# A list scheduler's rules in a two-layer diffusion backbone: which buffer, which rank, which order at the start

## The chip, the cores and the metric

The kernel runs on one core of a Trainium2 chip. The engines of a core each take their instructions in order: TensorE (PE, with its weight loads as PEld), VectorE (DVE), ScalarE (ACT), GpSimd (POOL) and SyncE (SP), which here only issues DMAs; ScalarE issues some too. The metric is the device time of one execution in microseconds.

## The reference

The input is 256 context tokens and 256 latent tokens of 1024 channels, in float32. Two layers change them; in each, a modulated RMS norm comes before an FFN, four token mixers (gated DeltaNet, Hyena, Mamba-2 SSD, GLA) and a second FFN. What matters of it:

```python
def pre_norm(t, gain, m, i):
    return modulate(rms_norm(t, gain), m[..., 3 * i, :], m[..., 3 * i + 1, :])

def swiglu(h, w_up, w_down):
    a, g = jnp.split(h @ w_up, 2, axis=-1)
    return (jax.nn.silu(a) * g) @ w_down
...
    for layer in range(DEPTH):
        mx = (cond_x @ w_ada[layer] + b_ada[layer]).reshape(b, 1, N_MOD, D_MODEL)
        mc = (cond_c @ w_ada[layer] + b_ada[layer]).reshape(N_MOD, D_MODEL)
        x = x + 0.5 * mx[..., 2, :] * swiglu(pre_norm(x, nw[0], mx, 0), ffn_up[layer, 0], ffn_down[layer, 0])
        yc, yx = token_mix(pre_norm(xc, nw[1], mc, 1), pre_norm(x, nw[1], mx, 1), w_in[layer], ...)
        x = x + mx[..., 5, :] * yx
        x = x + 0.5 * mx[..., 8, :] * swiglu(pre_norm(x, nw[2], mx, 2), ffn_up[layer, 1], ffn_down[layer, 1])
    return rms_norm(x, final_norm)
```

The context (xc) goes the same way with mc. The Hyena mixer needs filters that depend on weights alone: a small FFN, times a window, then a Fourier transform.

## The kernel before

**Tiling.** Activations lie with channels on the 128 partitions and tokens along them, as 128x512 tiles. Products are taken in a split form: a weight chunk `raw` is split into a high part `wh` (ScalarE, in the start GpSimd) and a rest `wl` (VectorE), an activation into `hh` and `hl`, and each product is three matmuls: wh with hh, wl with hh, wh with hl. `raw`, `wh` and `wl` have three buffers each.

**Norms.** A norm sums squares, turns the mean into a root by a chain of ten short VectorE steps on 128x4 values (`ms`, then `rq`, `rt`, `ru` by turns), spreads it to all partitions by a matmul with `rq`, and then makes for each of eight channel blocks `u` (VectorE, x times the root), `hh` (ScalarE) and `v` (GpSimd, two halves), and `hl` = v - hh (VectorE).

**Filters.** `G_unit` multiplies the output weights `hywo` of the filter FFN with its hidden values and windows them into `hSD`; `G_dft` transforms them into tiles `gA`, `gB` and a row `gn`, which SP stores to DRAM tensors `gdr`: all of gA, rows 1 to 127 of gA once more, gn and gB. Four of the norms (`norm_G`, L2153) mix these transforms with their own TensorE work, so that TensorE has something to do while the root is made. The modulation sums (`aa`, from weights `aw`) run on VectorE in between, over the whole kernel.

**Buffers.** `slot` (L609) gives a 128x512 tile of one pool of 34: u, v, hSD, gA, gB, gn, qkv, aw and more come out of it.

**Order.** Nothing is issued as the code is written. `body` runs against `Stand`, which records each operation with its engine, its dependences and a key: the sum of TensorE's time up to there (`self.t`), less an offset. `Plan` then walks through modelled time: of an engine's ready operations the one with the smallest key is next, and when an operation needs a new tile, the plan also picks which buffer of the pool it gets. `build` issues all operations in the plan's sequence, each buffer being a pool of its own with one place, and the tile framework adds the semaphore waits: an operation that writes into a buffer waits for the real end of the last one that used it. All planned instructions bear one line, L573, the call in `build`. `order` (L2445 on) makes the plan with a margin of 300 ns between engines.

Two calls in the kernel code, `manual_schedule(engines)` and `high_priority(offset)`, are recorded without effect in before: `manual_schedule` does nothing, and `high_priority` adds an offset of zero. They stand around `start()` (the loads, the first norm and the first product, for which all engines but SP were named), around the whole of `norm_G` (TensorE), in `wchunk` (L674, the splits of weight chunks) and in `gdn_proj`.

Of the kernel before, what the change touches and what calls it, by code (L numbers as in the profile page):

```python
# [10 lines left out]
F32 = mybir.dt.float32  # L11
# [125 lines left out]

class Op:  # L140

    __slots__ = ("n", "eng", "name", "args", "kw", "key", "deps", "left", "succ", "occ", "dur", "new", "tiles", "func", "ready", "dma", "start", "port")
# [7 lines left out]
class Stand:  # L150
# [3 lines left out]
    def __init__(self, nc):  # L154
        self.real, self.shadow = nc, _bacc.Bacc("TRN2", target_bir_lowering=False, num_devices=1)
        self.ops, self.tiles, self.hist, self.dr = [], {}, {}, set()
        self.t, self.off, self.pe_last, self.maker = 0.0, [0.0], {}, {}
        self.lane = ""
        for a, e in self.ENG.items():
            setattr(self, a, self.Engine(self, e))  # L160

# [22 lines left out]

    @contextlib.contextmanager
    def manual_schedule(self, engines=None):
        yield

    @contextlib.contextmanager
    def high_priority(self, offset=0):  # L190
        self.off.append(self.off[-1])
        yield
        self.off.pop()

# [35 lines left out]
    def note(self, eng, name, args, kw):  # L230
        if name == "preload_act_table_set":
            return Note()
        o = Op()
        o.n, o.eng, o.name, o.args, o.kw = len(self.ops), eng, name, args, kw
        o.dma = name == "dma_start"
        o.deps, o.succ, o.new, o.tiles = {}, [], None, []
        aps = [x for x in list(args) + list(kw.values()) if isinstance(x, bass.AP)]
        o.func = None
        for x in list(args) + list(kw.values()):
            if isinstance(x, type(AF.Copy)):  # L240
                o.func = x
        for i, x in enumerate(aps):
            tn, w = x.tensor.name, i == 0
            if tn in self.tiles:
                b = self.box(x)
                if tn not in o.tiles:
                    o.tiles.append(tn)
                    if tn not in self.hist:
                        assert w, (tn, name)
                        o.new, self.maker[tn] = tn, o.n  # L250
                    else:

                        o.deps.setdefault(self.maker[tn], -1)
            elif tn in self.dr:
                b = self.dbox(x)
            else:
                continue
            self.access(o, tn, w, b, tn in self.dr)
            if w and eng == "PE":
                p = self.pe_last.get(tn)  # L260
                if p is not None:
                    o.deps[p] = max(o.deps.get(p, 0), 0)
                self.pe_last[tn] = o.n
        for tn in o.tiles:
            self.tiles[tn][5] += 1
        self.cost(o, aps)
        o.key = self.t - self.off[-1]
        if eng == "PE":
            self.t += o.occ / 1e3
        self.ops.append(o)  # L270
        return Note()
# [86 lines left out]
class Plan:  # L358
# [10 lines left out]
    def run(self):  # L369
        st, ops = self.st, self.ops  # L370
# [39 lines left out]
        pend = {e: [] for e in engs}  # L410
        avail = {e: {} for e in engs}
        ft = {e: 0.0 for e in engs}
        table, dmaf, port = "S", 0.0, {"DVE": 0.0, "POOL": 0.0}
        G, posted = [], set()
        waiters = {}

# [12 lines left out]
        while G:  # L429
            t, e = heapq.heappop(G)  # L430
            posted.discard((t, e))
            if t < ft[e]:
                post(ft[e], e)
                continue
            while pend[e] and pend[e][0][0] <= t:
                o = ops[heapq.heappop(pend[e])[1]]
                c = st.tiles[o.new][0] if o.new else None
                heapq.heappush(avail[e].setdefault(c, []), (keys[o.n], o.n))
            best = None
            for c, h in avail[e].items():  # L440
                if not h:
                    continue
                k, n = h[0]
                if c is not None:

                    fr = free[c]
                    nf = sum(1 for f in fr if f[0] <= t)
                    i = nextpos[c]
                    if not nf or (pos[n] > i and slack[c][i:pos[n]].min() < 1):

                        m = self.order[c][nextpos[c]] if nextpos[c] < len(self.order[c]) else None
                        if nf and m is not None and m != n and (keys[m], m) in h:
                            k, n = keys[m], m
                        else:
                            later = [f[0] for f in fr if f[0] > t]
                            if later:
                                post(min(later), e)
                            waiters.setdefault(c, set()).add(e)
                            continue
                o = ops[n]  # L460
                if e == "ACT":
                    ta = table_of(o)
                    if ta and ta != table:
                        k += self.swap
                if best is None or k < best[0]:
                    best = k, n, c
            if best is None:
                if pend[e]:
                    post(max(pend[e][0][0], ft[e]), e)
                continue  # L470
            _, n, c = best
            o = ops[n]
            h = avail[e][c]
            if h[0][1] == n:
                heapq.heappop(h)
            else:
                h.remove((keys[n], n))
                heapq.heapify(h)
            if c is not None:
                fr = free[c]  # L480
                f = max((x for x in fr if x[0] <= t), key=lambda x: x[0])
                fr.remove(f)
                self.slot[o.new] = f[1]
                done_new.add(n)
                slack[c][nextpos[c]:pos[n]] -= 1
                l = self.order[c]
                while nextpos[c] < len(l) and l[nextpos[c]] in done_new:
                    nextpos[c] += 1
                    for x in waiters.pop(c, ()):
                        post(t, x)  # L490
            occ, dur = o.occ, o.dur
            if e == "ACT":
                ta = table_of(o)
                if ta and ta != table:
                    table = ta
                    occ, dur = occ + 1283, dur + 1283
            o.start = t
            if o.port:
                x = 0.7 * max(0.0, min(port["POOL" if e == "DVE" else "DVE"] - t, dur))
                occ, dur = occ + x, dur + x  # L500
                port[e] = t + dur
            ft[e] = t + occ
            if o.dma:
                b = max(t + occ, dmaf)
                dmaf = b + dur / 230.0
                end = dmaf + 2300
            else:
                end = t + dur
            seq.append(n)
            n_done += 1  # L510
            for s in o.succ:
                x = ops[s]
                if x.deps[n] < 0:
                    r = t + 1
                elif x.deps[n] == 0 and x.eng == e:
                    r = t + occ
                elif x.eng == e and not o.dma:
                    r = end if e != "PE" else t + occ
                else:
                    r = end + self.LAT[x.eng] + self.margin  # L520
                x.ready = max(x.ready, r)
                x.left -= 1
                if not x.left:
                    push(x)
            for tn in o.tiles:
                left[tn] -= 1
                endt[tn] = max(endt[tn], end)
                if not left[tn]:
                    c2 = st.tiles[tn][0]
                    free[c2].append((endt[tn] + 60, self.slot[tn]))  # L530
                    for x in waiters.pop(c2, ()):
                        post(max(endt[tn] + 60, ft[x]), x)
            post(ft[e], e)
# [46 lines left out]
class Kern:  # L580
# [44 lines left out]
        self.nc.sync.dma_start(s[:, t:], d[:, t:])  # L625
        return s

    def small(self, shape, s="sm", dt=F32, bufs=8):
        return self.pt.tile(list(shape), dt, name=self.nm(s), tag="sm%d" % int(np.prod(shape[1:])), bufs=bufs)

    def psum(self, tag="mm", shape=(128, 512)):
# [1811 lines left out]


def order(st):  # L2445
    plan = Plan(st, {}, 300.0, 8.0)
    if plan.stuck:
        raise RuntimeError("no order found")
    return plan


def body(nc, tc, I, O):
    from contextlib import ExitStack
    with ExitStack() as es:
        K = Kern(nc, tc, I, es)
        with tc.manual_schedule(engines={mybir.EngineType.PE, mybir.EngineType.DVE, mybir.EngineType.Activation, mybir.EngineType.Pool}):
            acts = K.start()
        K.ada_it, K.ada_done = K.ada(), (0, 1)
        with tc.issue_after(K.last_ld.ins):
# [58 lines left out]
```

## Time and profile before

| | us |
|---|---|
| median of three runs | 2789.42 |
| lowest and highest | 2787.28, 2791.71 |
| the profiled execution | 2792.31 |
| its span, first to last instruction | 2790.5 |
| TensorE busy, idle | 2656.2, 134.3 |
| VectorE, ScalarE, GpSimd busy | 1894.4, 1049.6, 360.4 |

The mean granted TensorE clock over the span is 0.976 of 2.4 GHz. The rows below come from the page of the profile, from lists of who waited for whom, from the chain of work that ended last (each piece is what released the next), from lists of instructions in order of time, and from busy times by stretch. In a list in order of time, the number in front is the start in us, the second the time until the end of the last instruction of the piece, and the brackets hold the idle time of the engine ahead of the piece and what ended it.

### The profile page before, as it was taken

The numbers are of one execution on the slowest core, as the hardware profiler recorded it, in microseconds if no ns is written. First come the engines' busy times: TensorE is split into PE (matmuls) and PEld (weight loads), VectorE is DVE, ScalarE is ACT, GpSimd is POOL, SyncE is SP. The second block draws the span as 40 slices with busy tenths as digits, with TensorE's granted clock in tenths as the row PEclk, the third lists the DMA queues.
The fourth block names the chain that finished last, engine by engine and source line by source line (L and its number), as shares of the span: only waits on it lengthen the run. The fifth ranks groups of instructions, "written<-read, shape, count | busy, mean of one in ns | idle before, by whom it ended". The sixth has DMA issues, their size and how long they took to land.

```text
span 2790.5 us, 40144 instructions
## 1 busy us (share of the span) xinstructions
PE 2656.2 (95%) x15131; PEld 2279.0 (82%) x15131; DVE 1894.4 (68%) x3783; ACT 1049.6 (38%) x1603; POOL 360.4 (13%) x439
## 2 busy tenths in 40 slices
PE   3999998899999999998999998999989999999998
PEld 2788876688989888886888877888868899999998
DVE  3978873679867565588637668376347988777555
ACT  1322222554433543233222223222237435644443
POOL 1200000201121243421000001000013012222000
PEclk7999999999999999999999998999989999999999
DMA  8655543243344233254534544344224445555454
GB/s 239 191 172 185 180 141 115 62 114 84 106 134 143 75 104 105 76 167 154 163 98 151 151 135 152 106 151 138 92 79 119 133 122 149 177 163 182 152 183 142
DMA packets 369698, 382.67 MB, mean 137 GB/s; under 512 B 43466, under 2 KB 317544, under 8 KB 369504
## 3 DMA queue, kind: packets, MB, share of 16 engines
q1 hardware_dynamic: 347568, 363.67, 43.1%
q10 hardware_dynamic: 21936, 16.44, 1.9%
q8 instruction: 119, 1.95, 0.3%
q14 instruction: 75, 0.61, 0.1%
HBM read 355.79 MB, written 24.25 MB: 136 GB/s over the span
## 4 chain that ended last, share of the span: by engine, by line
PE 86%; DVE 6%; DMA 5%; issue 1%; ACT 1%; SPq 1%; POOL 1%; ACTq 0%; DVEq 0%
PE pmm L573 74%; PE px L573 12%; DMA gdr<-gA 2%; DVE qkv L573 1%; DVE aa L573 1%; DVE wl L573 1%; SPq L573 1%; DMA gdr<-gn 1%; DVE xbc L573 1%; POOL bm L573 0%; DMA aw<-in_w_ada 0%; DVE x L573 0%; DMA win<-in_hywin 0%; DVE TC L573 0%; DVE u L573 0%
## 5 line engine op out<-in xcount | busy, mean ns | idle before, releaser
L573 PE MATMUL pmm<-hh,wh 128*128 128x512 f32 (+1 forms) x2464 | 895.9, 364 | 24.7 <-ACT hh L573 17.6
L573 ACT ACTIVATE wh<-raw 128x1024 fp32r<-128x1024 f32 (+1 forms) x480 | 501.5, 1046 | 1100.9 <-PE pmm L573 1044.4
L573 DVE TENSOR_TENSOR wl<-raw,wh 128x1024 fp32r<-128x1024 f32 (+1 forms) x486 | 600.7, 1237 | 462.1 <-ACT wh L573 437.0
L573 PE MATMUL pmm<-hh,wl 128*128 128x512 f32 (+1 forms) x2464 | 888.7, 361 | 1.6 <-DVE wl L573 1.5
L573 PE MATMUL pmm<-hl,wh 128*128 128x512 f32 (+1 forms) x2464 | 883.3, 360 | 5.2 <-DVE hl L573 5.2
L573 PEld LDWEIGHTS pmm<-hh,wh 128*128 128x128 f32 x2464 | 470.4, 191 | 99.7 <-ACT hh L573 18.5
L573 PEld LDWEIGHTS pmm<-hl,wh 128*128 128x128 f32 x2464 | 468.3, 190 | 74.4 <-DVE hl L573 5.9
L573 PEld LDWEIGHTS pmm<-hh,wl 128*128 128x128 f32 x2464 | 470.7, 191 | 67.9 <-DVE wl L573 2.1
L573 DVE SCALAR_TENSOR_TENSOR aa<-aw,cond,aa 128x256 f32<-128x256 f32 x896 | 374.0, 482 | 1.7 <-DMA aw<-in_w_ada 1.6
L573 PE MATMUL pmm<-ah,wh 128*128 128x512 f32 (+1 forms) x704 | 257.3, 366 | 0.6 <-DVE sil L573 0.6
L573 PE MATMUL pmm<-ah,wl 128*128 128x512 f32 (+1 forms) x704 | 255.6, 363 | 0.0
L573 PE MATMUL pmm<-al,wh 128*128 128x512 f32 (+1 forms) x704 | 255.6, 363 | 0.0
L573 PEld LDWEIGHTS pmm<-ah,wh 128*128 128x128 f32 x704 | 133.1, 189 | 24.4 <-issue 2.5
L573 PEld LDWEIGHTS pmm<-al,wh 128*128 128x128 f32 x704 | 133.0, 189 | 21.1 <-issue 0.4
L573 PEld LDWEIGHTS pmm<-ah,wl 128*128 128x128 f32 x704 | 133.1, 189 | 20.3
L573 POOL TENSOR_SCALAR v<-u,Am,mods 128x256 f32<-128x256 f32 x72 | 56.1, 795 | 514.7 <-DVE u L573 472.4
L573 PE MATMUL pmm<-wh,hh 128*128 128x256 f32 x416 | 120.2, 289 | 0.0
L573 PE MATMUL pmm<-wl,hh 128*128 128x256 f32 x416 | 119.3, 287 | 0.0
L573 PE MATMUL pmm<-wh,hl 128*128 128x256 f32 x416 | 118.8, 286 | 0.0
L573 PE MATMUL pmm<-yh,wh 128*128 128x512 f32 (+1 forms) x256 | 87.6, 343 | 0.0
L573 PE MATMUL pmm<-yl,wh 128*128 128x512 f32 (+1 forms) x256 | 86.3, 340 | 0.0
L573 PE MATMUL pmm<-yh,wl 128*128 128x512 f32 (+1 forms) x256 | 86.1, 337 | 0.0
(383 smaller groups left out, 3396.8 us busy)
## 6 DMA issues: line engine op xcount, KB each, us to landing
raw<-in_ffn_up SPq DMA_DIRECT2D x172, 512.0 KB
raw<-in_w_in SPq DMA_DIRECT2D x164, 512.0 KB
aw<-in_w_ada SPq DMA_DIRECT2D x288, 256.0 KB
raw<-in_ffn_down SPq DMA_DIRECT2D x80, 512.0 KB
raw<-in_w_branch SPq DMA_DIRECT2D x32, 512.0 KB
fe<-pk SPq DMA_DIRECT2D x42, 256.0 KB
raw<-in_w_out SPq DMA_DIRECT2D x16, 512.0 KB
pk<-pj ACTq DMA_DIRECT2D x26, 256.0 KB
```

Of the source, the lines that this page charges most:

```text
L573: getattr(engines[o.eng], o.name)(*[sub(a) for a in o.args], **{k: sub(v) for k, v in o.kw.items()})
```

## The change

The operations, their number and their sizes stay as they are. What changes is how the plan is made:

- `manual_schedule` takes effect: the operations of each named engine inside it are chained in the order in which the code states them. SP is now named too at `start()`, and after that block no operation gets a key below the TensorE time at its end (`floor`).
- `high_priority` lowers the key by 15 us (`lead`): the splits of weight chunks and the raw copies of `gdn_proj` rank that much earlier.
- A new tile gets the buffer that has been free longest, not the one that became free last.
- Of two dependent operations on one engine (DVE, ACT, POOL) the second may be planned as soon as the engine has taken the first (`occ`), not at its end.
- Each DMA queue has a modelled rate of its own, 290 B/ns for SP and 100 for ScalarE; before, both shared 230.
- The margin between engines is 200 ns, not 300, and small tiles have 6 buffers, not 8.

```diff
     def manual_schedule(self, engines=None):
+        self.strict = {NAMES[e]: None for e in engines}
         yield
+        if "SP" in self.strict:
+            self.floor = self.t
+        self.strict = {}
...
     def high_priority(self, offset=0):
-        self.off.append(self.off[-1])
+        self.off.append(self.off[-1] + self.lead)
...
+        if eng in self.strict:
+            if self.strict[eng] is not None:
+                o.deps.setdefault(self.strict[eng], -1)
+            self.strict[eng] = o.n
...
-        o.key = self.t - self.off[-1]
+        o.key = max(self.t - self.off[-1], self.floor)
...
                 fr = free[c]
-                f = max((x for x in fr if x[0] <= t), key=lambda x: x[0])
+                f = min(fr)
...
-                b = max(t + occ, dmaf)
-                dmaf = b + dur / 230.0
-                end = dmaf + 2300
+                b = max(t + occ, dmaf[e])
+                dmaf[e] = b + dur / (290.0 if e == "SP" else 100.0)
+                end = dmaf[e] + 2300
...
                 elif x.eng == e and not o.dma:
-                    r = end if e != "PE" else t + occ
+                    r = t + occ
...
-    def small(self, shape, s="sm", dt=F32, bufs=8):
+    def small(self, shape, s="sm", dt=F32, bufs=6):
...
-    plan = Plan(st, {}, 300.0, 8.0)
+    plan = Plan(st, {}, 200.0, 8.0)
...
-        with tc.manual_schedule(engines={mybir.EngineType.PE, mybir.EngineType.DVE, mybir.EngineType.Activation, mybir.EngineType.Pool}):
+        with tc.manual_schedule(engines={mybir.EngineType.PE, mybir.EngineType.DVE, mybir.EngineType.Activation, mybir.EngineType.Pool,
+                                         mybir.EngineType.SP}):
```

How it moves instructions, at three places. A row is an instruction with its tiles (a name, the number of the tile and a running number) and, in brackets, the semaphores that it waits for; DMAHW0 to 7 are those of DMAs.

VectorE in the norm ahead of the first FFN of layer 1 (norm_G(1,0), near 1680 us; x a token tile, px the spread root), before:

```order
L573 TENSOR_TENSOR u2679_14332<-x2092_10723,px2678_14318 128x512 [waits DMAHW1_49,PE_49]
L573 TENSOR_TENSOR u2680_14339<-x2093_10746,px2678_14318 128x512 [waits DMAHW7_49]
L573 TENSOR_TENSOR u2681_14349<-x2104_10782,px2678_14318 128x512
L573 TENSOR_TENSOR u2682_14354<-x2105_10805,px2678_14318 128x512
L573 TENSOR_TENSOR u2687_14363<-x2122_10838,px2678_14318 128x512 [waits DVE_49,Activation_49,Pool_49]
L573 TENSOR_TENSOR hl2684_14371<-v2685_14345,hh2683_14343 128x512
L573 TENSOR_TENSOR u2691_14383<-x2123_10863,px2678_14318 128x512
L573 TENSOR_TENSOR u2695_14391<-x2134_10889,px2678_14318 128x512 [waits DMAHW7_49]
L573 TENSOR_TENSOR u2699_14398<-x2135_10918,px2678_14318 128x512 [waits DMAHW6_49,DMAHW5_49,DMAHW4_49]
```

and of the change:

```order
L585 TENSOR_TENSOR u2679_14303<-x2092_10706,px2678_14285 128x512 [waits PE_49]
L585 TENSOR_TENSOR u2680_14306<-x2093_10729,px2678_14285 128x512
L585 TENSOR_TENSOR u2681_14315<-x2104_10776,px2678_14285 128x512
L585 TENSOR_TENSOR u2682_14321<-x2105_10796,px2678_14285 128x512
L585 TENSOR_TENSOR hl2684_14329<-v2685_14311,hh2683_14309 128x512 [waits Activation_49,Pool_49]
L585 MEMSET gB2674_14323 1x256 [waits Activation_49]
L585 TENSOR_TENSOR u2687_14343<-x2122_10831,px2678_14285 128x512
L585 TENSOR_TENSOR u2691_14353<-x2123_10850,px2678_14285 128x512
L585 TENSOR_TENSOR u2695_14361<-x2134_10885,px2678_14285 128x512
L585 TENSOR_TENSOR u2699_14370<-x2135_10902,px2678_14285 128x512
```

The eight u stand in nearly the same row; the four waits for DMAs are no longer there.

VectorE in the middle of the first FFN (near 430 us; hSD windowed filters, win the window, hyb a bias row), before:

```order
L573 COPY gn634_3679<-px633_3665 1x256 [waits DMAHW1_49,DMAHW2_49,DMAHW0_49,PE_49]
L573 TENSOR_TENSOR hSD642_3690<-px641_3681,win1_173 128x512 [waits DMAHW4_49,DVE_49,PE_49]
L573 MEMSET gB631_3684 1x256 [waits Activation_49]
L573 TENSOR_TENSOR hSD642_3690<-hSD642_3690,hyb611_3525 1x256 [waits DVE_49]
L573 TENSOR_TENSOR hSD644_3700<-px643_3687,win1_173 128x512 [waits DMAHW3_49,PE_49]
L573 TENSOR_TENSOR hSD653_3715<-px652_3692,win1_173 128x512 [waits DMAHW6_49,DMAHW7_49,DMAHW5_49,PE_49]
L573 TENSOR_TENSOR hSD655_3720<-px654_3702,win1_173 128x512 [waits DMAHW0_49,PE_49]
```

and of the change:

```order
L585 COPY gn634_3651<-px633_3643 1x256 [waits PE_49]
L585 TENSOR_TENSOR hSD642_3667<-px641_3660,win1_136 128x512 [waits PE_49]
L585 MEMSET gB631_3662 1x256 [waits DMAHW1_49,DMAHW2_49,DMAHW0_49,Activation_49]
L585 TENSOR_TENSOR hSD642_3667<-hSD642_3667,hyb611_3536 1x256 [waits DVE_49]
L585 TENSOR_TENSOR hSD644_3679<-px643_3665,win1_136 128x512 [waits DMAHW3_49,PE_49]
L585 TENSOR_TENSOR hSD653_3702<-px652_3695,win1_136 128x512 [waits DMAHW6_49,DMAHW5_49,DMAHW7_49,DMAHW4_49,PE_49]
L585 TENSOR_TENSOR wl686_3706<-raw684_3449,wh685_3697 128x1024 [waits Activation_49]
L585 TENSOR_TENSOR hSD653_3702<-hSD653_3702,hyb617_3571 1x256 [waits DVE_49]
L585 TENSOR_TENSOR hSD655_3721<-px654_3700,win1_136 128x512 [waits DMAHW7_49,PE_49]
```

The three DMA waits have gone from gn634 to the zeroing of gB631, those of hSD653 are there in both, and a weight rest wl686 now stands behind it.

SP's loads in the start, before, the 44th to the 53rd (raw22 is the first chunk of the first product's weights, here its second half):

```order
L573 DMA hyb216_179<-in_hy_bias 1x256
L573 DMA hyb218_181<-in_hy_bias 1x256
L573 DMA hywo215_175<-in_hy_wout 64x256
L573 DMA hywo217_177<-in_hy_wout 64x256
L573 DMA aw70_264<-in_w_ada 128x4x128
L573 DMA aw85_266<-in_w_ada 128x4x128
L573 DMA aw86_270<-in_w_ada 128x4x128
L573 DMA raw22_126<-in_ffn_up 128x2x256
L573 DMA raw31_128<-in_ffn_up 128x2x256
L573 DMA raw71_146<-in_ffn_up 128x2x256
```

and of the change, the 26th to the 34th:

```order
L585 DMA hywo215_138<-in_hy_wout 64x256
L585 DMA hywo217_140<-in_hy_wout 64x256
L585 DMA hyb216_144<-in_hy_bias 1x256
L585 DMA hyb218_146<-in_hy_bias 1x256
L585 DMA hywo215_138<-in_hy_wout 64x256
L585 DMA hywo217_140<-in_hy_wout 64x256
L585 DMA raw22_106<-in_ffn_up 128x2x256
L585 DMA aw23_259<-in_w_ada 128x4x128
L585 DMA aw24_261<-in_w_ada 128x4x128
```

The second half of raw22 has gone from the 51st place to the 32nd, ahead of the modulation weights aw23 and later, which were ahead of it.

## Rows read from the trace of the kernel before

**Rows 1.** The page: TensorE's busy time, and the shares of the chain that ended last.

```profile
PE 2656.2 (95%) x15131; PEld 2279.0 (82%) x15131; DVE 1894.4 (68%) x3783; ACT 1049.6 (38%) x1603; POOL 360.4 (13%) x439
...
PE 86%; DVE 6%; DMA 5%; issue 1%; ACT 1%; SPq 1%; POOL 1%; ACTq 0%; DVEq 0%
```

**Rows 2.** For whom TensorE waits, whole span: us in total, times, longest.

```profile
PE pmm L573 <- ACT hh L573: 17.6, 3, 10.1
PE px L573 <- DVE hl L573: 13.8, 2, 9.4
...
PE px L573 <- DVE gn L573: 7.7, 1, 7.7
PE px L573 <- POOL v L573: 6.2, 1, 6.2
...
PE pmm L573 <- DVE hl L573: 5.2, 1, 5.2
PE px L573 <- DVE hSD L573: 4.6, 1, 4.6
```

**Rows 3.** The same view, from 2100 us to the end.

```profile
PE pmm L573 <- ACT hh L573: 1.2, 1, 1.2
```

**Rows 4.** The tensors gdr: who waited for their DMAs (us, times).

```profile
  DVE u L573: 44.7, 6
  POOL v L573: 23.7, 2
```

**Rows 5.** The chain that ended last, 488 to 520 us: start us, us, what.

```profile
493.73 18.29 DMA gdr<-gA
...
512.14 0.10 DVE u L573
```

**Rows 6.** Instructions in order of time, VectorE, from 1676 us.

```profile
1676.10 3.08 DVE L573 TENSOR_TENSOR u<-x,px 128x512 f32<-128x512 f32 x5 [6.86 <-DMA gdr<-gB]
...
1688.54 1.28 DVE L573 TENSOR_TENSOR u<-x,px 128x512 f32<-128x512 f32 x2 [8.16 <-DMA gdr<-gn]
```

**Rows 7.** The same view, GpSimd, from 2072 us.

```profile
2072.85 12.15 POOL L573 TENSOR_SCALAR v<-u,Am,mods 128x256 f32<-128x256 f32 x16 [17.37 <-DMA gdr<-gn]
```

**Rows 8.** Busy time by stretch (us, PE, PEld, DVE, ACT, POOL; PEclk, DMA share, GB/s).

```profile
100.00:400.00 300.00, 300.00 (x1378) 243.16 (x1377) 257.69 (x561) 82.32 (x104) 1.20 (x2) 1.00 0.59 179
480.00:500.00 20.00, 16.53 (x97) 12.10 (x95) 7.30 (x24) 4.04 (x8) 0.62 (x1) 0.99 0.40 130
500.00:524.00 24.00, 16.83 (x53) 11.29 (x54) 11.89 (x18) 10.55 (x19) 12.19 (x16) 0.72 0.07 24
1276.00:1300.00 24.00, 13.95 (x59) 11.20 (x58) 13.68 (x27) 9.06 (x17) 12.85 (x16) 0.79 0.26 80
1676.00:1700.00 24.00, 16.84 (x52) 12.91 (x53) 12.89 (x20) 9.41 (x18) 12.88 (x16) 0.69 0.14 45
2060.00:2084.00 24.00, 11.30 (x35) 7.50 (x35) 11.53 (x27) 8.68 (x17) 11.15 (x16) 0.57 0.12 45
```

**Rows 9.** Instructions in order of time in the start: split, first product, next chunk.

```profile
59.05 1.05 POOL L573 TENSOR_SCALAR wh<-raw 128x1024 fp32r<-128x1024 f32 x1 [19.85 <-DMA raw<-in_ffn_up]
...
70.14 0.50 PE L573 MATMUL pmm<-hh,wh 128*128 128x512 f32 x1
...
98.83 0.50 PE L573 MATMUL pmm<-hh,wh 128*128 128x512 f32 x1 [1.03 <-ACT sil L573]
```

**Rows 10.** The same view, SP: the issue of the last block's modulation weights.

```profile
69.74 2.91 SPq L573 DMA_DIRECT2D aw<-in_w_ada  x4
```

**Rows 11.** Busy time by stretch, the first 100 us (columns as in Rows 8).

```profile
0.00:100.00 100.00, 53.16 (x434) 40.39 (x435) 50.03 (x121) 27.27 (x48) 28.49 (x41) 0.83 0.77 221
```

**Rows 12.** The instructions on wl alone, by stretch (us, PE, PEld, DVE; PEclk, DMA share, GB/s).

```profile
550.00:1250.00 700.00, 330.78 (x912) 172.14 (x911) 131.55 (x99) 1.00 0.37 110
...
2100.00:2600.00 500.00, 267.17 (x892) 172.31 (x893) 135.57 (x108) 0.98 0.49 146
```

**Rows 13.** For whom VectorE waits, whole span: us in total, times, longest.

```profile
DVE wl L573 <- PE pmm L573: 6.8, 8, 2.3
```

More of the change, by code (lines that the diff above doesn't have):

```diff
@@ L136 @@
 GS = {(0, 1): (3, 1), (0, 2): (2, 2), (1, 0): (3, 2), (1, 1): (2, 2)}
+NAMES = {mybir.EngineType.PE: "PE", mybir.EngineType.DVE: "DVE", mybir.EngineType.Activation: "ACT", mybir.EngineType.Pool: "POOL", mybir.EngineType.SP: "SP"}
 class Op:
@@ L157, in __init__ @@
         self.t, self.off, self.pe_last, self.maker = 0.0, [0.0], {}, {}
-        self.lane = ""
+        self.strict, self.lead, self.floor = {}, 15.0, 0.0
         for a, e in self.ENG.items():
@@ L412, in run @@
         ft = {e: 0.0 for e in engs}
-        table, dmaf, port = "S", 0.0, {"DVE": 0.0, "POOL": 0.0}
+        table, dmaf, port = "S", {"SP": 0.0, "ACT": 0.0}, {"DVE": 0.0, "POOL": 0.0}
         G, posted = [], set()
```

## The prediction

> **What bounds the kernel now.** I read the page first: TensorE is busy 2656.2 of 2790.5 us, and the chain that ended last is 86% TensorE, 6% VectorE and 5% DMA [rows 1]. The change neither adds nor removes a matmul, so what it can win is the 134 us in which TensorE is idle, and what the lower clock costs behind such pauses. Next I read for whom TensorE waits. Some 40 us lie in the first 100 us; nearly all the rest lies in five places, which I call T1 (near 430 us, in the middle of the first FFN, where filters are made) and T2 to T5 (near 505, 1280, 1680 and 2070 us, the four norms that norm_G writes). The rows are 7.7 + 4.6 = 12.3 us for T1, and 17.6 + 13.8 + 6.2 + 5.2 = 42.8 us for T2 to T5 [rows 2], of which 1.2 us belong to another place, late in the span [rows 3]: 41.6 us.
>
> The engine that a row names is only the last link. Who waits for the stores to gdr tells more: u on VectorE 44.7 us in 6 waits, v on GpSimd 23.7 us in 2 [rows 4]. Now u and v read nothing of gdr, and gdr<-gA and gdr<-gn are stores out of buffers. So this is reuse: u was given a buffer out of which a filter was still being stored. The chain at T2 shows it in order of time: the store of 127 rows of gA takes 18.29 us, and u starts as it ends [rows 5]. At T4, u waits 6.86 us for the store of gB and later 8.16 us for that of gn [rows 6]; at T5, v waits 17.37 us [rows 7].
>
> **The change, part by part.**
>
> 1. *Longest free buffer first.* Before, a new tile takes the buffer that became free last in the plan's time. The plan lets a store of 256 KB end some 3.4 us after its issue (bytes at 230 B/ns and 2.3 us), where the trace has up to 18.29 us [rows 5]. So the buffers of which the plan is most wrong are the first to be given out again. After, the one that has been free longest is given out, and the order listings show what comes of it: at T4 the four waits of u for a DMA are gone, and so they are for u at T2, T3 and T5. Of 22 tiles of the norms and filters that followed a store into its buffer, 6 are left: five at T1, and one v at T2 with 48 matmuls between.
>    - Idle time. At T4 the first u would start at 1676.10 - 6.86 = 1669.2 us, and TensorE, which stood 6.3 us there, would hardly stop. Were all of it so, 41.6 us would go. Late next is v: 16 of them take 12.15 us [rows 7], 0.76 each, and two make a block of hl, 1.5 us. A block feeds twelve matmuls; at 300.00 us for 1378 of them [rows 8] that is 12 x 0.22 = 2.6 us. So GpSimd keeps ahead after the first block, but the chain from the root of the mean square over u, hh and v to the first matmul remains. The nearest row for a pause with no such wait in it is 480 to 500 us: 3.5 us idle [rows 8]. Between none and 3.5 us for each place I take 2, 8 in all, since T4 shows none and the root's own chain must be somewhere: **-34 us** (bounds -41.6; and -20, if half only turns into waits for v and for the root).
>    - Clock. In 24 us at each of T2 to T5 the granted clock is 0.72, 0.79, 0.69 and 0.57, with TensorE busy for 16.83, 13.95, 16.84 and 11.30 us [rows 8]. Busy time by 1 - clock is what full clock would have saved: 4.7 + 2.9 + 5.2 + 4.9 = 17.7 us. The stretch with 3.5 us idle has 0.99, so a pause of that size can leave the clock up. I take two thirds: **-12 us** (bounds -17.7 and -4).
>    - T1: **0** (4 us either way). The listing shows the waits in other places, but not fewer: gn is free of them and the zeroing of gB has them, and hSD still waits for four queues. ScalarE and VectorE now have a split of weights queued behind these waits, and TensorE sixteen more matmuls of the down projection to do meanwhile.
>
> 2. *First stage in the stated order.* Before, the weights of the first product are split only at 59.05 us, when their second half has landed, and that product starts at 70.14 us [rows 9]; this half is the 51st load of SP, with 12.1 MB ahead of it. The stage's matmuls are done just before 98.83 us, where the next chunk starts [rows 9]. After, the half is the 32nd load with 7.4 MB ahead, and the first product can start some 25 us earlier. But in stated order each block of the product waits for the modulation two blocks on, and the last block's modulation weights are now SP's 80th load, at 20.5 MB, not the 70th, at 17.6: loads of later stages go between. Before, these last four were issued from 69.74 to 72.65 us [rows 10], so SP's queue moved 17.6 MB in 72.65 us, 243 GB/s. At that pace 20.5 MB take 84.5 us; 2 us for the landing; and behind it stand 32 small matmuls and three blocks of twelve, 36 x 0.22 = 7.9, some 9 us together. The stage ends at 95.5 us and not at 98.8: **-3 us**. At the plan's own 290 B/ns it would be 82 us, -17; at the 221 GB/s that all queues together moved in the first 100 us [rows 11], 93 + 9 = 102 us, +3. I take the pace of SP's own queue, since it is the queue in question.
>    The plan now gives SP's and ScalarE's queues a rate each, 290 and 100 B/ns, where it had 230 for both; the trace has 221 GB/s for both together [rows 11]. The Trainium skill (DMA: Bandwidth & Descriptors, Issuing engines are not separate DMA queues) says that what several engines issue runs on the same 16 DMA engines and interleaves, which speaks against this part. The trace agrees so far as 221 is below either sum. By that rule loads come later than planned and this term would be +3 in place of -3, the whole gain 6 us less.
>
> 3. *Splits ranked 15 us earlier, dependent work back to back, margin 200 in place of 300 ns, six small buffers in place of eight.* The work is the same, and in the mixers no row of weight lets TensorE wait, so there is nothing to win; what it may cost is a rival below. The root's steps in one piece may give a us at T3 and T4, which is inside the 2 us above. **0.**
>
> **Sum.** -34 - 12 + 0 - 3 = -49 us. The profiled execution took 2792.3 us, 2.9 us over the median; the terms are differences, so I take them from the median, 2789.4: **2740 us**, -1.8%. With all bounds: -41.6 - 17.7 - 4 - 17 = -80, 2709; and -20 - 4 + 4 + 3 = -17, 2772.
>
> **The rivals.**
>
> *Half of it turns into other waits* (2762 us). u is free to start, but the chain of the root, the sixteen v and the sums of the modulation that VectorE does in between set the pace; TensorE pauses 4 to 5 us at each place, and the clock falls nearly as before: -20 - 4 - 3 = -27. For it: the 3.5 us idle between 480 and 500 us, which no store causes [rows 8]. Against it: at T4 the wait of u is longer than TensorE's whole pause.
>
> *The change does not do what it says* (2788 us). The 34 buffers may be so nearly full at these places that the longest free is hardly older than the last, and its store still under way. For it: T1, where this is so. Against it: the listings at T2 to T5, which hold whatever the times are.
>
> *Slower: splits hold up the mixers.* wh and wl have three buffers each. A split ranked 15 us ahead of its use comes to its engine while its buffer is still being read; the engine stands, and behind it stand the short dependent steps of the mixers, for which TensorE waits. From 550 to 1250 and from 2100 to 2600 us there are 99 + 108 = 207 splits [rows 12]. If each held TensorE up by 0.24 us, all of the 49 us would be gone; from 0.27 us on the kernel is measurably slower, and at 0.4 us, 83 us, it is at 2823. For it: VectorE has waited in front of wl for matmuls, 6.8 us in 8 times [rows 13]. Against it: that is 0.85 us for 8 of 486, none of which TensorE felt, and the plan places a split only when it believes the buffer free.
>
> *More* (2714 us). T1 goes as well, since sixteen matmuls more cover its 12 us, and the start ends near its bound, 14 us better than I have it: -49 - 12 - 14 = -75.
>
> **How the numbers follow.** The forecast has 0.54 (own range 2722 to 2758), half of it 0.20, more 0.12, no effect 0.06, slower 0.08. A range of 8 in 10 reaches from the lowest bound, 2709, past "half of it" to 2780; it leaves out the slower case, most of "no effect" and the edge of "more". About 0.2%, 5.6 us, is what a measurement of this kernel can tell from no change: faster by more 0.86, within 0.05, slower 0.09.
>
> **What the profile after would show.** Right: no wait of u or v for gdr near 505, 1280, 1680 and 2070 us, two or three us idle at each, and a granted clock of 0.9 and above in those 24 us; the same two waits at T1, one of them now in front of ScalarE's gB; the first product near 45 us, with pauses in it until some 87 us, and the next chunk at 94 to 98. Wrong: u as late as before, but for the broadcast of the root (half of it); waits for gdr under other names, qkv or sil, with TensorE behind them; or wl and wh waiting for TensorE in the mixers, and TensorE busy for less than 0.98 of the stretch from 550 to 1250 us (slower). The forecast fails at its root if a store of gA is still the last thing before the first matmul at T2.

## The result and the profile after

The changed kernel takes 2760.5 us in the median, the kernel before 2790.6 in the same runs: a ratio of 0.9894, 95% interval 0.9877 to 0.9912. It is faster by 30 us, where 49 were forecast; 2760.5 lies inside the range, 2.5 us above the forecast's own range of 2722 to 2758, and a little short of "half of it" at 2762. But it didn't come about as that rival says, as the stretches show.

The page of the profile after, span and busy times:

```profile
span 2759.9 us, 40079 instructions
...
PE 2661.1 (96%) x15131; PEld 2275.8 (82%) x15131; DVE 1910.1 (69%) x3783; ACT 1043.5 (38%) x1598; POOL 359.4 (13%) x439
```

Who waited for the stores to gdr after [rows 4 before] (us, times):

```profile
  ACT gB L585: 10.7, 1
  DVE hSD L585: 9.8, 1
```

No u and no v is left in the list. The two that are left are T1's. Busy time after, in 24 us at T1 and at T2 to T5 (columns as in rows 8):

```profile
420.00:444.00 24.00, 20.90 (x91) 16.07 (x90) 8.36 (x15) 5.72 (x8) 0.00 (x0) 0.86 0.30 99
490.00:514.00 24.00, 23.46 (x117) 17.93 (x116) 18.11 (x38) 11.72 (x21) 9.71 (x13) 1.00 0.30 91
1268.00:1292.00 24.00, 23.03 (x112) 17.85 (x112) 21.33 (x43) 12.88 (x23) 13.15 (x16) 1.00 0.37 116
1648.00:1672.00 24.00, 23.29 (x106) 18.15 (x104) 21.67 (x44) 12.90 (x23) 12.90 (x16) 1.00 0.41 129
2030.00:2054.00 24.00, 20.24 (x82) 14.23 (x82) 16.28 (x36) 13.50 (x25) 12.72 (x17) 0.85 0.16 48
```

The last four answer to [rows 8]: TensorE idles 0.5, 1.0, 0.7 and 3.8 us where it idled 7.2, 10.1, 7.2 and 12.7, and the clock is full in three of four. So these stalls are gone as forecast. What came in their place stands in the list of whom TensorE waits for after [rows 2]:

```profile
PE px L585 <- DMA aw<-in_w_ada: 17.2, 8, 13.8
PE pmm L585 <- DVE wl L585: 11.7, 4, 8.8
PE px L585 <- ACT qkv L585: 7.0, 5, 2.6
PE px L585 <- DVE Y L585: 6.6, 6, 2.9
...
PE px L585 <- ACT gB L585: 3.1, 1, 3.1
```

The modulation weights (aw) are the start. The waits for wl, qkv and Y (the last two belong to the gated DeltaNet) lie in the mixers; the kernel before has 1.5, 1.7 and 2.4 us of them. The time at which TensorE spreads the root of each norm cuts the span in stages that can be compared between kernels (us; worked out from the lists in order of time, of one profiled execution for each kernel; the mixers of layer 0 lie between T2 and T3, those of layer 1 between T5 and the last norm):

| kernel | T2 | T3 | T4 | T5 | last norm | end | T2 to T3 | T5 to last |
|---|---|---|---|---|---|---|---|---|
| before | 493.3 | 1276.5 | 1667.6 | 2062.5 | 2584.5 | 2790.5 | 783.2 | 522.0 |
| after | 482.7 | 1268.0 | 1648.4 | 2030.6 | 2554.2 | 2759.9 | 785.4 | 523.6 |
| e1 | 483.1 | 1251.7 | 1633.8 | 2012.1 | 2522.6 | 2728.2 | 768.6 | 510.5 |
| e2 | 482.0 | 1264.1 | 1645.8 | 2026.9 | 2534.0 | 2739.7 | 782.1 | 507.1 |
| e5 | 478.3 | 1257.6 | 1637.7 | 2019.2 | 2544.0 | 2749.4 | 779.3 | 524.8 |
| e7 | 475.9 | 1257.6 | 1639.8 | 2017.5 | 2525.1 | 2729.3 | 781.8 | 507.6 |
| e8 | 476.5 | 1245.8 | 1628.2 | 2006.8 | 2520.4 | 2725.7 | 769.3 | 513.6 |
| e11 | 473.3 | 1241.8 | 1623.6 | 2001.8 | 2515.3 | 2721.0 | 768.6 | 513.5 |

After against before: 10.7 us are won up to T2, 10.7 from T3 to T4, 12.8 from T4 to T5. But the two stages with the mixers, which begin with T2 and T5, are 2.2 and 1.6 us longer, though some 15 and 11 us of stall and clock are gone from them. So about 17 and 13 us are lost again inside the two mixers. That is what the experiments are for. (e1 below has the buffer rule alone; against it the two stages are 16.8 and 13.1 us longer, which is the same sum.)

### The profile page after: what moved, and what is told of

It is laid out like the page before. It is cut to its first block, busy times and chain, and to the rows that moved or that the text cites. A ratio compares the mean times of both kernels' runs of the same rounds, so it can differ in the third digit from the quotient of the medians.

```text
span 2759.9 us, 40079 instructions
## 1 busy us (share of the span) xinstructions
PE 2661.1 (96%) x15131; PEld 2275.8 (82%) x15131; DVE 1910.1 (69%) x3783; ACT 1043.5 (38%) x1598; POOL 359.4 (13%) x439
## 4 chain that ended last, share of the span: by engine, by line
PE 83%; DVE 10%; DMA 3%; issue 1%; POOL 1%; ACT 1%; SPq 0%; ACTq 0%; DVEq 0%; POOLq 0%
PE pmm L585 72%; PE px L585 11%; DVE qkv L585 1%; DVE wl L585 1%; DVE X L585 1%; DVE P L585 1%; DVE xbc L585 1%; DVE aa L585 1%; DMA raw<-in_ffn_up 1%; DMA aw<-in_w_ada 0%; DVE u L585 0%; DMA gdr<-gA 0%; POOL bm L585 0%; POOL v L585 0%; DVE TC L585 0%
## 5 line engine op out<-in xcount | busy, mean ns | idle before, releaser
L585 PEld LDWEIGHTS pmm<-ah,wl 128*128 128x128 f32 x704 | 133.5, 190 | 20.6
L585 PEld LDWEIGHTS pmm<-wl,hh 128*128 128x128 f32 x416 | 80.1, 193 | 9.4 <-DVE wl L585 9.0
```

The source lines that it names most:

```text
L585: getattr(engines[o.eng], o.name)(*[sub(a) for a in o.args], **{k: sub(v) for k, v in o.kw.items()})
```

## The experiments

All medians are timed against the kernel before (2790.2 to 2791.0 us in these runs); the intervals of the ratios are some 0.003 wide, 4 us either way. Each edit makes a new plan, which also moves stages that it does not mean by up to 3 us (e6 against e2, for one), so that much is not read as an effect. Five times lie 0.1 to 1.6 us outside the range of the theory that they speak for (e1, e2, e3, e7 and e9), and that of e4 lies far outside.

**e1: the buffer rule alone**, on the kernel before.

```diff
-                f = max((x for x in fr if x[0] <= t), key=lambda x: x[0])
+                f = min(fr)
...
-    def small(self, shape, s="sm", dt=F32, bufs=8):
+    def small(self, shape, s="sm", dt=F32, bufs=6):
```

> The kernel before with the longest-free buffer rule alone (and six small buffers, which that rule needs to fit). Between the spread of the root in the norms, the change took 10.7 us off T3 and its FFN and 12.8 us off T4 and its FFN, but the two stages that begin with T2 and T5 and hold the mixers came out 2.2 and 1.6 us longer, though their waits for the stores are gone: some 16 us are lost inside each of the two mixers. Theory A (back-to-back planning of dependent steps makes VectorE's chains in the mixers look shorter than they are): this kernel keeps all four gains and loses nothing in the mixers, 2790.6 - 14 - 11 - 13 - 14 = 2739 us (2733 to 2748). Theory B (splits and raw copies ranked 15 us earlier do it): the same 2739. Theory C (the buffer rule itself moves the waits into the mixers): 2790.6 - 24 = 2767 us.

Measured: 2731.7 us, 0.9787 (0.9772 to 0.9801). The rule alone is worth 59 us, twice the whole change. The mixers' stages are 14.6 and 11.5 us shorter than before and not longer, so C falls: the loss in the mixers isn't the buffer rule's. The other parts together cost 29 us. At T1 the stall is still there:

```profile
PE px L573 <- DVE gn L573: 6.7, 1, 6.7
```

**e2: the change without the back-to-back rule.**

```diff
-                    r = t + occ
+                    r = end if e != "PE" else t + occ
```

> The changed kernel, but a dependent step on the same engine is planned from the end of the step before it, as in the kernel before. Theory A: TensorE's waits between 560 and 720 and between 2100 and 2300 us go, 20 to 32 us less than the change: 2730 to 2740 us. Theories B and C: as the change, 2760 us, 5 either way.

Measured: 2741.6 us, 0.9826 (0.9809 to 0.9842), 19 us under the change, for A. Nearly all of it, 16.5 us, is in the mixers of layer 1; in those of layer 0 only 3.3 us come back.

**e3: the change with no lead.**

```diff
-        self.strict, self.lead, self.floor = {}, 15.0, 0.0
+        self.strict, self.lead, self.floor = {}, 0.0, 0.0
```

> The changed kernel with no lead: splits and raw copies rank as in the kernel before. Theory B: 20 to 32 us less than the change, 2730 to 2740 us. Theories A and C: 2760 us, 5 either way.

Measured: 2765.8 us, 0.9910 (0.9895 to 0.9924), 5 us over the change. B falls: splits that rank 15 us earlier do no harm, and if anything they help a little. With it falls the forecast's slower rival, which had put its price on them.

**e4: the change with the old buffer rule** (e1's first line the other way).

> The changed kernel with the old buffer rule, the one freed last. All theories that hold the buffer rule for the gain at T2 to T5: the waits for stores come back, 2760.5 + 35 to 50 = 2795 to 2810 us under A and B, since the loss in the mixers stays; under C that loss goes too and it is near 2780 us, the start's gain of 10 us below the kernel before.

Measured: 2832.9 us, 1.0151 (1.0136 to 1.0166). The range was missed upwards, by 23 us over its end. Without the buffer rule, the rest of the change makes the kernel slower by 42 us. Two of the waiters for gdr here:

```profile
  POOL v L585: 77.5, 3
  DVE u L585: 24.4, 3
```

With hSD (20.6 us, 2), gA (11.9, 1) and gn (8.1, 1) these are ten waits, as many as in the kernel before (u 6, v 2, gn 1, hSD 1), but 142.5 us of idle time ahead of them in place of 88.4. So the waits are not more here, but longer. Which of the other parts does that wasn't tried.

**e5: buffer rule and back-to-back rule**, on the kernel before.

> The kernel before with the longest-free rule (2731.7 us by itself) and the back-to-back rule. In the changed kernel, taking the back-to-back rule out gave 19 us, 16.5 of it in the mixers of layer 1. If the rule does that by itself, it costs the same here: 2745 to 2755 us, with the stretch from the fifth to the sixth spread of the root some 16 us longer than 510.5. If it only hurts together with the other changes: 2728 to 2737 us.

Measured: 2748.7 us, 0.9853 (0.9839 to 0.9868). Back-to-back costs 17 us by itself. The stage from T5 to the last norm has 524.8 us against 510.5, 14 more; that from T2 to T3 has 11 more, and 5 us are won before T2.

**e6: e2 with the old margin of 300 ns.**

> The changed kernel without the back-to-back rule (2741.6 us) and with the old margin of 300 ns. It has 13.5 us more than the longest-free rule alone between the second and third spread of the root (the mixers of layer 0: 782.1 against 768.6 us). Theory D, the smaller margin plans hand-overs too early there: 2728 us, 2 either way, that stretch at 769. Theory E, the stated order in the norms and the start does it: as without, 2741 us, 4 either way.

Measured: 2742.1 us, 0.9825 (0.9809 to 0.9841). D falls; the margin is worth nothing that can be seen.

**e7: e2 without the stated order.**

```diff
     def manual_schedule(self, engines=None):
-        self.strict = {NAMES[e]: None for e in engines}
         yield
```

> The changed kernel without the back-to-back rule (2741.6 us) and without the stated order: manual_schedule does nothing again, at the start and in the norms. Theory E: the mixers of layer 0 return to 769 us, and since the start gains nothing by the second spread (482 us with the stated order, 483 without), the whole is at 2728 us, 3 either way. Theory D: 2741 us, 4 either way.

(After the start's block `floor` is no longer set either.) Measured: 2731.1 us, 0.9791 (0.9777 to 0.9806): the total of E, 10 us under e2, but not in E's place. The mixers of layer 0 stay at 781.8 us; 6 us are won before T2 and 4 behind it, in small pieces. In the first 100 us, e2 and e7:

```profile
0.00:100.00 100.00, 62.37 (x454) 43.64 (x455) 65.81 (x166) 29.35 (x51) 34.95 (x42) 0.76 0.80 243
```

```profile
0.00:100.00 100.00, 66.92 (x477) 46.42 (x478) 64.45 (x146) 29.58 (x52) 26.21 (x42) 0.80 0.78 234
```

Busy time by granted clock, 62.37 x 0.76 = 47.4 us of full-clock work against 66.92 x 0.80 = 53.5. Without the stated order TensorE has done 6 us more of its work by then.

**e8: the kernel before with the store in two.** No rule of the plan is touched.

```diff
-            nc.sync.dma_start(dr[2][1:], A[1:])
+            nc.sync.dma_start(dr[2][1:113], A[1:113])
+            nc.sync.dma_start(dr[2][113:], A[113:])
```

> The kernel before, and only the store of rows 1 to 127 of gA made as two, of 112 and of 15 rows. No rule of the plan changes. If the stalls are there because this one store takes 18 us where the store of 128 rows takes a few, and the buffers are reused meanwhile, then this alone takes nearly all of what the longest-free rule takes, T1 too: 2725 to 2740 us. If the stores are late for another reason (a busy queue, many small pieces), it takes less than a third: 2775 us or more.

Measured: 2727.5 us, 0.9777 (0.9762 to 0.9791), 63 us: twice the change, by one line of the kernel itself. At T1, gn again in a buffer of gA:

```profile
416.71 0.41 DVE L573 COPY gn<-px 1x256 f32<-1x256 f32 x1 [2.62 <-DMA gdr<-gA]
```

It waits 2.62 us for the store where it waited long enough for TensorE to stand 7.7 us behind it [rows 2]. So the reuse of the buffer was harmless where the store is short; the shape of the store made the stall. The Trainium skill (DMA: Bandwidth & Descriptors, Why a DMA increments its semaphore by 16 and not by 1) says that a DMA is spread over the largest number of engines, up to 16, that divides the slowest dimension of both its sides: a 127-row tile goes to one engine. By that rule 112 rows go to 16 and 15 rows to 15. For the 127 rows the trace of the kernel before agrees. At T2, while TensorE stands, the last two columns (DMA share and GB/s) show one of 16 DMA engines at work:

```profile
497.00:500.00 3.00, 0.00 (x0) 0.00 (x0) 0.00 (x0) 0.00 (x0) 0.00 (x0) 0.96 0.06 25
```

At 25 GB/s the 254 KB of one such store take some 10 us. For the 112 and the 15 rows no view used here tells the engines apart.

The long store also holds up SP, whose longest issue of a store of gA takes 9.6 us before and 1.4 us here. That is not what cost the time: in e1 it is still 9.7 us, and 59 us are gone.

**e9: the change with true times for back-to-back steps.**

```diff
+                w = max([endof[d] + 40 - t for d, k in o.deps.items() if k > 0 and ops[d].eng == e and d in endof] + [0.0])
+                occ, dur = occ + w, dur + w
```

> The changed kernel, dependent steps still ranked back to back, but the plan now books the time that a step really waits for the one ahead of it: to its end and 40 ns more, 0.455 us a step of the triangular solve (128x256) where the back-to-back rule books 0.351 and the trace of the change has 0.46. Theory A1, the rule costs because the plan's times for such chains are too short, so what stands behind them comes too late: 2738 to 2745 us, as without the rule. Theory A2, it costs because dependent steps stand in a row and VectorE stands still for 0.1 us at each: 2757 to 2764 us, as the change, since the row is the same (684 steps behind the one they need, 685 in the change, 306 without the rule).

Measured: 2765.4 us, 0.9911 (0.9897 to 0.9926), no better than the change. A1 falls: knowing the true time doesn't help as long as the steps stand in a row. A2's range ended at 2764. Its longest wait for wl is even longer than the change's 8.8 us:

```profile
PE pmm L591 <- DVE wl L591: 14.6, 3, 10.5
```

What the row does is seen in the mixers of layer 1. VectorE in the change, the triangular solve of the DeltaNet (P from L and X, then X less P), in order of time, and ScalarE's wh beside it:

```profile
2138.50 1.22 DVE L585 TENSOR_TENSOR wl<-raw,wh 128x1024 fp32r<-128x1024 f32 x1
...
2141.31 0.42 DVE L585 TENSOR_TENSOR P<-L,X 128x255 f32<-128x255 f32 x1
2141.77 0.42 DVE L585 TENSOR_TENSOR X<-X,P 128x255 f32<-128x255 f32 x1
...
2152.40 1.22 DVE L585 TENSOR_TENSOR wl<-raw,wh 128x1024 fp32r<-128x1024 f32 x1
```

```profile
2138.82 1.05 ACT L585 ACTIVATE wh<-raw 128x1024 fp32r<-128x1024 f32 x1
...
2153.68 0.58 PE L585 MATMUL pmm<-wl,hh 128*128 128x256 f32 x1 [8.77 <-DVE wl L585]
```

From 2139.6 to 2152.4 us VectorE does nothing but the solve, each step 0.46 us after the other at first, and less as the tiles get narrower. The next wl could have been made at 2139.9, when its wh was there; it comes 12.5 us later, and TensorE stands for 8.77. The same place in e2:

```profile
2137.76 0.42 DVE L585 TENSOR_TENSOR X<-X,P 128x255 f32<-128x255 f32 x1
2138.10 1.22 DVE L585 TENSOR_TENSOR wl<-raw,wh 128x1024 fp32r<-128x1024 f32 x1
2139.24 0.41 DVE L585 TENSOR_TENSOR P<-L,X 128x252 f32<-128x252 f32 x1
...
2140.47 1.22 DVE L585 TENSOR_TENSOR wl<-raw,wh 128x1024 fp32r<-128x1024 f32 x1
```

Here the splits go in between two steps. When a dependent step is ready only at the end of the one ahead, the plan has the engine free a moment earlier, and gives that moment to the next ready thing. When it is ready at once and has the smaller key, the chain isn't broken into. The plan of the change shows this for the late wl: it is ready at 2078.4 us of modelled time and taken at 2086.9, since its key is 2024.3 and the 31 steps of the solve in between, each ready as the one ahead is taken, have keys from 2000.0 to 2016.6. Busy time shows the second cost: in the mixers of layer 1, e2 and the change,

```profile
2027.00:2534.00 507.00, 489.27 (x3620) 455.55 (x3618) 414.50 (x863) 265.83 (x441) 110.02 (x139) 0.98 0.49 146
```

```profile
2030.00:2554.00 524.00, 492.40 (x3620) 455.27 (x3619) 425.60 (x863) 267.57 (x441) 116.38 (x139) 0.99 0.47 141
```

the same 863 VectorE instructions take 11 us more, and in the plan 255 of them stand behind the one whose result they need, not 108. The two go together: in the rows above an instruction that needs nothing of the one ahead starts some 0.08 us before that one ends (wl at 2138.10, the end of X at 2138.18), one that does starts 0.04 us after, and 147 x 0.08 us are an estimated 12. How much of the 16.5 us is the chain that can't be broken and how much these 11 us isn't separated by any run; but TensorE's idle time in these stretches is 31.6 us in the change and 17.7 in e2, and 9.6 and 0.5 us of it are waits for wl.

**e10: e2 with the stated order at the start only.**

> The changed kernel without the back-to-back rule, with the stated order at the start alone and not in the four norms. With both it has 2741.6 us, with neither 2731.1. If the start holds the loss (its first product waits for modulation weights that come late): 2738 to 2743 us, the second spread of the root near 482 us. If the norms hold it: 2730 to 2734 us, that spread near 476 us.

Measured: 2738.3 us, 0.9813 (0.9796 to 0.9829), T2 at 483.4. The start holds 7 of the 10 us, the norms 3, which is no more than a new plan moves.

**e11: e1 and e8 together**, on the kernel before.

> The kernel before with the longest-free rule (2731.7 us alone) and the store in two (2727.5 us alone). Both take the waits for the 127 rows away, so they add only where the rule has left them: at T1, where 6.7 us and some clock remain under the rule: 2720 to 2726 us. If they were two different gains of 59 and 63 us they would add up to 2670 us.

Measured: 2721.7 us, 0.9754 (0.9740 to 0.9769). The two don't add up: 59 and 63 us make 69, so they remove the same stalls, and the store alone takes T1.

**e12: e7 and e8 together.**

> The parts that have paid: longest-free buffer, lead of 15 us, a rate for each DMA queue, margin 200 ns, without the back-to-back rule and without the stated order (2731.1 us so far), and the store in two, which takes T1's wait of 7 us and its clock: 2720 to 2726 us. If the store brings nothing here because the loads at the start hold that stretch: 2729 to 2733 us.

Measured: 2722.2 us, 0.9754 (0.9739 to 0.9768). e11 and e12 beat both kernels, by 2.5% and 1.4%, and are not to be told apart. Without the back-to-back rule and the stated order, the lead, the queues' rates and the margin come to nothing in the sum.

## Why the prediction was right, and where it was off

The cause and the largest term were right. That the time lies in the range is in part luck: the range reaches to 2780 for the sake of "half of it", which did not happen, and 12 us won beyond the forecast, at T1 and T2, set off part of the 30 lost in the mixers.

**The cause, and the rule's part (term 1): right.** u and v waited for a buffer out of which a filter was being stored; e1 and e8 show it from two sides. Idle time at T2 to T5 fell from 37.1 to 6.0 us in the 24-us stretches, where 8 us were expected to stay, and the clock's loss by the forecast's own sum from 17.7 to 20.24 x 0.15 = 3.0 us, where it was to stay at 5.7. So the -34 and -12 were -31 and -15, the same -46. Some 3 us more of T2's stall lie outside its 24 us and are gone as well.

Three readings under it were off. The first is the row on which the text built what would stay, the 3.5 us idle between 480 and 500 us, "which no store causes". They are the start of T2's own stall, from 496.5 us on, and u stood there behind a store:

```profile
500.76 3.08 DVE L573 TENSOR_TENSOR u<-x,px 128x512 f32<-128x512 f32 x5 [7.46 <-DMA gdr<-gn]
...
502.72 0.66 PE L573 MATMUL px<-hh,wh 128*64 128x512 f32 x1 [6.19 <-POOL v L573]
```

The granted clock of 0.99 in that stretch is not what such a pause leaves behind either: from 500 to 506 us it is 0.50. So the 3.5 us, between which and none the text chose its 2, and the two thirds of the clock had no row under them; that both came near is in part luck. The second is the 18.29 us at T2 [rows 5], which are not the store of 127 rows alone. By the trace they begin with the issue of the last of the three stores of gA, a single row, and up to 500 us the 127 rows of the filter ahead still run, at the 25 GB/s that e8 shows; a store of 127 rows by itself takes some 10 us. The third: "nearly all the rest lies in five places" holds for 54 of 87 us: of the 134 us idle, 47 lie in the first 100 us and 54 at T1 to T5, but 15.8 in the mixers of layer 1 (2084 to 2584 us), in pieces of up to 2.9 us, and 9.9 behind them.

**T1: wrong place for the zero.** The store is waited for as forecast, twice, the first time in front of ScalarE's gB:

```profile
422.90 0.60 ACT L585 ACTIVATE gB<-px 128x512 f32<-128x512 f32 x1 [10.73 <-DMA gdr<-gA]
423.55 2.08 PE L585 MATMUL px<-hywo,hym 128*128 128x256 f32 x4 [3.10 <-ACT gB L585]
...
434.52 0.69 DVE L585 TENSOR_TENSOR hSD<-px,win 128x512 f32<-128x512 f32 x1 [9.77 <-DMA gdr<-gn]
```

But TensorE stands 3.1 us in all, not 12.3. Matmuls of the down projection, which the text names, cover the rest: those from 415.8 to 419.4 us part of the first wait, those from 425.1 us on the whole of the second. The term was 0, 4 either way, and measured some -9; the rival "more" had it.

**The start (term 2): the loads as forecast, the end not.** The first product starts at 52.3 us, not near 45, because its modulation comes late. The last modulation weights hold it until 87.69 us, where the sum has 84.5 + 2 = 86.5. But the stage ends later than before: the next chunk starts at 101.08 us, not at 95.5, and before at 98.83 [rows 9].

```profile
43.32 2.93 PE L585 MATMUL px<-aw,cond 128*32 128x128 f32 x32 [13.80 <-DMA aw<-in_w_ada]
...
52.26 0.80 PE L585 MATMUL pmm<-hh,wh 128*128 128x512 f32 x1
...
87.69 0.43 PE L585 MATMUL px<-aw,cond 128*32 128x128 f32 x8 [0.58 <-DMA aw<-in_w_ada]
...
90.74 0.50 PE L585 MATMUL pmm<-hl,wh 128*128 128x512 f32 x1 [1.97 <-DVE hl L585]
...
101.08 0.50 PE L585 MATMUL pmm<-hh,wh 128*128 128x512 f32 x1
```

The three blocks behind those weights take 13 us and not 9: TensorE waits 1.97 us for hl in them, and has a granted clock of 0.87 from 88 to 101 us. (The sum's upper bound also leaves out its own 2 us for the landing: at 221 GB/s it comes to 93 + 2 + 9 = 104 us, +5 and not +3.) TensorE did other work meanwhile. By 100 us it has done 62.77 x 0.71 = 44.6 us of full-clock work, against 53.16 x 0.83 = 44.1 before [rows 11]:

```profile
0.00:100.00 100.00, 62.77 (x443) 43.16 (x444) 64.49 (x157) 28.12 (x49) 33.23 (x42) 0.71 0.78 238
```

That is a term of 0 to -1 for a forecast -3, inside its bounds of -17 and +3. What the text did not see is that the plan without a stated order does better by 6 us (e7): it priced the stated order against the kernel before alone. The queues moved 238 GB/s together, which lies between the two rates weighed there.

**Term 3: the step that failed.** "The work is the same, and in the mixers no row of weight lets TensorE wait, so there is nothing to win"; and for the price it looked at the splits alone. The back-to-back rule was put at zero with "a us at T3 and T4", and it costs 17 to 19 us (e2, e5); the stated order, which is term 2's, costs 10 (e7), of which 7 are the start's. The trace of before gave a hint: VectorE has its long dependent chains in the mixers, and TensorE idles only 3.1 us there in layer 0 (524 to 1276 us), so that a new rule for ranking had little to win and an order to spoil. The plan showed it too, with 685 against 290 VectorE rows that stand right behind the row they need; the text looked only at the norms and the start.

**Sum.** -46, T2's 3 more, T1's -9 and the start's -1 make -59 us; the mixers give back 17 + 13 = 30 of it, and what is left is -29, measured -30. Of the 30 that the mixers give back, the back-to-back rule has some 19 (e2); the rest is open. **The rivals:** "half of it" had the number (2762) and not the mechanism: the norms gave everything, and half was spent elsewhere. "Slower" had the place, the mixers, with the wrong part of the change. Its check, TensorE busy below 0.98 between 550 and 1250 us, gave the alarm rightly: 15.5 of the 700 us are idle, 0.978.

**Open:** the mixers of layer 0 take 11 to 16 us longer in e2, e6, e7 and e12 than in e1 and e11, and in e7 and e12 nearly as much is won ahead of T2 and in layer 1. In e7 TensorE idles 11.9 us between T2 and T3, most of it for Y (3.7) and vn (3.5), where it idles 3.5 in e1. In e5 the back-to-back rule alone has 11 us there, so the two causes overlap and don't add. Of the parts that e2, e6, e7 and e12 have in common the margin (e6) is cleared, and taking out the lead won nothing beside the back-to-back rule (e3); neither the lead nor the rates of the two DMA queues were tried alone.

## What to carry to other kernels

Before the reuse of a buffer is changed, look at why the old user held it so long: one line that shapes a store for all engines was worth as much as the new rule, and more than the whole change. Where a scheduler picks buffers, the one free longest forgives a wrong model of the transfers; and a rule that ranks dependent steps back to back should be tried alone, since it shuts out the splits that another engine waits for.

## What the runs showed of the hardware

Stores of 127 rows of 2 KB moved at 25 GB/s, with a DMA share of one engine of 16 (e8), some 10 us each; at T2 two such stores, one behind the other, made the 18.29 us [rows 5]. After each was made as 112 and 15 rows, the instruction behind it at T1 waited 2.62 us in place of 11.68 (e8), and the kernel was 63 us faster. Two dependent VectorE steps of 128x255 elements start 0.46 us apart with 0.42 us each; in e2 a split of 1.22 us between two of them makes it 1.48 us from step to step, 1.0 us more and less than its own length.
